# A transformer-style layer on one core: second parts of the query weights kept in DRAM between two groups of tokens, and the buffers of the dense expert pass laid out anew

## The chip, the cores and the metric

The kernel runs on one core of a Trainium2 chip. The metric is the time of one execution in microseconds (us) on the device. An engine is named as in the profile: PE is the matrix engine (TensorE), PEld its weight loads, DVE the vector engine, ACT the scalar engine, POOL GpSimd, and SP the sync engine, which here only issues DMAs. PEclk is the clock that PE was granted, as a share of its full speed.

## The reference, cut to what matters

One layer over 9 tiles of 128 tokens (one tile of context, eight of latent tokens), width 1024, all in fp32. Two mixers, an output projection and a gated residual come first. The part that the change touches is the last one, a product-key lookup over 128 x 128 single-neuron experts:

```
h = rmsnorm(x, norm2_g) * (1.0 + scale2) + shift2
q = (h @ w_q).reshape(n_tok, 8, 2, 128)            # 8 heads, two halves
s = einsum('thpc,hpkc->thpk', q, sub_keys)         # 128 scores per half
v1, i1 = top_k(s[:, :, 0], 16) ; v2, i2 = top_k(s[:, :, 1], 16)
top_v, top_j = top_k(v1[..., :, None] + v2[..., None, :], 16)
idx = i1 * 128 + i2 at top_j ; g = softmax(top_v)
a = gelu(einsum('bd,bed->be', h, u_tab[idx])) * g  # 128 experts per token
x = x + gate2 * einsum('be,bed->bd', a, v_tab[idx])
```

## The kernel before, in words

**Products.** A weight comes in units of 128 x 1024 floats (512 KB). `load_unit` (L147) loads one into a slot of `wraw` on SP's queue; `split` (L98) makes of it a first part `wH` (ACT, a rounded copy, L99) and a second part `wL` (DVE, the difference, L100). `mmx` (L124) then multiplies two such pairs with three matmuls: H by H (L129), H by L or L by H (L130, L131). `unit` (L181) does load and split in one; `wH` and `wL` have two buffers each.

**Stages.** After the mixers the latent tiles go in two groups of four through `group`: GA (tiles 5 to 8), then GB (tiles 1 to 4). A group does its output projection, the second norm, and then the *q stage*, a loop over 16 units of query weights (units 60 to 75 of the list, `u + 44 + b`): 24 matmuls `pq`, an ACT copy `qs`, four matmuls `psc` with the keys, and on DVE `top16` for each of the four tiles (L414 to L420: MAX, MAX_INDEX, MATCH_REPLACE, MAX, MAX_INDEX). Both groups read the same 16 units and split them again. When a group has its scores, `combine` chooses the 16 best pairs of each head.

**Two ways to use the experts.** Tiles 0 to 3 gather the rows of their experts: an indirect DMA on POOL's queue for each of 128 experts per token row (`gu`, `gv`), and a DVE instruction for each (`jk`, L814; `acc`, L829). Tiles 5, 6, 7, 8 and 4 (DENSE) take all experts in a dense pass. For that, a *build* turns a tile's choice into a matrix G in DRAM (`G_d`): one-hot rows on DVE and ACT, matmuls `pG`, ACT copies `Gs` (L563), writes by SP (L567). Tile 4 is in GB, so its choice and its build come last, directly ahead of the dense pass. The dense pass runs e over 128 groups of 128 experts: `hidden` (48 matmuls `pH` of 320 columns and a GELU on ACT) gives `a`; DVE multiplies `a` by a slice `Gt` of G (L1078) and splits it into `aH`, `aL`; `out_res` adds 18 matmuls `pout` for three tiles into PSUM; every fourth e `out_rot` does 48 matmuls `prot` for two tiles, added to `accd` on DVE. For each e a unit of u and one of v are loaded (`ur`, `vr`) and split. Group e's Gt comes for four e at a time, in five pieces, one for each tile.

**Order.** A scheduler lays the instructions of each engine out ahead of the run by priorities and by when buffers come free; every engine then runs its list in order. Work of the gather is let into DVE's list by `anchor` and `paced` (L104 to L114): a gather instruction may not stand ahead of the split that was recorded some units before. Ahead of the dense pass the two units u0 and u1 go through `unit` and their `pH` run before the build. Then the pools of the groups are closed and a pool `dp` is opened in their place, whose buffers (`raw`, `uH`, `uL`, `vH`, `vL`, `a`, `aH`, `aL`, `Gt`, `accd`) can be filled when what lay there before is done.

## Time and profile before

| | us |
|---|---|
| three runs | 3621.89, 3634.37, 3636.42; median 3634.37 |
| profiled execution, its own time | 3629.96 |
| span in the profile | 3628.2 |
| GA's q stage | about 940 to 1040 |
| GB's q stage, to the last top16 | about 1528 to 1657 |
| choice of tile 4, second half | 1657 to 1671.5 |
| build of tile 4 | 1671.5 to 1713 |
| dense pass | 1713 to 3606 |

The span is cut into stages by the names of the instructions. The profiled execution lies 4.4 us below the median of the three runs. PE is busy for 3336.8 us of the span, DVE for 2817.6, ACT for 1121.3, POOL for 1429.2. A busy share is an average over stages with different limits; the rows further below are taken stage by stage.

### The profile page before, as it was taken

Reading aid. Unit: us, or ns where it says so; the run is one execution under the profiler, and the core shown is the slowest. Engines: PE = TensorE matmul, PEld = TensorE weight load, DVE = VectorE, ACT = ScalarE, POOL = GpSimd, SP = SyncE. Lnnn points to the kernel's source line nnn. Section 1 sums busy time; section 2 is a strip of 40 time slices with the busy share of each in tenths; the row PEclk is TensorE's granted clock in tenths of the full one; section 3 lists DMA queues with packets and bytes.
Section 4 is the critical chain, followed back from the end, with each engine's and each line's share of the span. In section 5 each row is a group of like instructions: output and inputs, shape, how many; then the busy total and the mean of one; then the engine's idle time right before and its main releaser. Section 6 shows DMA issues by size and latency. Waiting matters only on the chain. (4 is left out here: it accounts for less than half of the span.)

```text
span 3628.2 us, 48825 instructions
## 1 busy us (share of the span) xinstructions
PE 3336.8 (92%) x17547; PEld 2764.3 (76%) x17547; DVE 2817.6 (78%) x5427; ACT 1121.3 (31%) x2095; POOL 1429.2 (39%) x1128
## 2 busy tenths in 40 slices
PE   8898999899887999877889999989999999999997
PEld 4386888775665676666788898889898888898996
DVE  2317678785899888697888888888887888788887
ACT  2512443321323655625322222222222222222222
POOL 0102102553112322200365664655555456555653
PEclk9899999999999999999999999999999999999998
DMA  7787324789534778643898997998998799988986
GB/s 282 287 294 274 113 72 132 257 313 342 168 127 141 271 255 325 248 144 117 291 332 299 326 327 268 336 326 306 324 319 320 245 343 333 324 305 316 337 320 247
DMA packets 361957, 971.12 MB, mean 268 GB/s; under 512 B 32721, under 2 KB 142673, under 8 KB 356081
## 3 DMA queue, kind: packets, MB, share of 16 engines
q0 software_dynamic: 149824, 546.37, 42.4%
q1 hardware_dynamic: 211888, 421.62, 33.6%
q8 instruction: 138, 2.26, 0.3%
q14 instruction: 107, 0.87, 0.1%
HBM read 897.07 MB, written 70.80 MB: 267 GB/s over the span
## 5 line engine op out<-in xcount | busy, mean ns | idle before, releaser
L811 POOL DMA_INDIRECT gu<-in_urow_dram,ix x512 | 688.2, 1344 | 1004.7 <-DVE jk L814 421.9
L824 POOL DMA_INDIRECT gv<-in_vrow_dram,ix x512 | 687.3, 1342 | 819.5 <-DVE acc L829 412.2
L814 DVE SCALAR_TENSOR_TENSOR jk<-gu,h2r 128x1024 f16<-128x1024 f32 x512 | 625.2, 1221 | 127.9 <-DMA gu<-in_urow_dram,ix 121.8
L829 DVE SCALAR_TENSOR_TENSOR acc<-gv,act,acc 128x1024 f32<-128x1024 f32 x508 | 651.3, 1282 | 45.2 <-DMA gv<-in_vrow_dram,ix 37.5
L129 PE MATMUL pH<-h2DH,uH 128*128 128x320 f32 x2016 | 626.5, 311 | 10.6 <-DVE accd L1061 8.2
L131 PE MATMUL pH<-h2DH,uL 128*128 128x320 f32 x2016 | 623.7, 309 | 1.1 <-DVE uL L100 1.1
L130 PE MATMUL pH<-h2DL,uH 128*128 128x320 f32 x2016 | 624.2, 310 | 0.0
L129 PEld LDWEIGHTS pH<-h2DH,uH 128*128 128x128 f32 x2016 | 380.4, 189 | 21.7 <-DVE accd L1061 13.4
L130 PEld LDWEIGHTS pH<-h2DL,uH 128*128 128x128 f32 x2016 | 380.4, 189 | 4.5
L131 PEld LDWEIGHTS pH<-h2DH,uL 128*128 128x128 f32 x2016 | 380.2, 189 | 1.7 <-DVE uL L100 1.7
L129 PE MATMUL pout<-vH,aH 128*128 128x512 f32 x768 | 300.6, 394 | 21.9 <-ACT vH L99 16.1
L99 ACT ACTIVATE vH<-vr 128x1024 fp32r<-128x1024 f32 x128 | 133.2, 1058 | 564.0 <-DMA vr<-in_vrow_dram 295.8
L131 PE MATMUL pout<-vH,aL 128*128 128x512 f32 x768 | 301.7, 393 | 4.1 <-DVE aL L100 4.1
L130 PE MATMUL pout<-vL,aH 128*128 128x512 f32 x768 | 301.7, 393 | 1.1 <-DVE vL L100 1.1
L129 PE MATMUL prot<-vH,aH 128*128 128x512 f32 x512 | 209.2, 409 | 54.4 <-DVE accd L1061 50.1
L99 ACT ACTIVATE wH<-wraw 128x1024 fp32r<-128x1024 f32 x118 | 124.9, 1058 | 401.9 <-PE pq L130 163.7
L100 DVE TENSOR_TENSOR vL<-vr,vH 128x1024 fp32r<-128x1024 f32 x128 | 156.1, 1220 | 91.0 <-ACT vH L99 90.9
L560 PE MATMUL pG<-oh 128*128 128x128 f16 x1280 | 176.8, 316 | 33.3 <-ACT Gs L563 21.6
L560 PEld LDWEIGHTS <-oh 128*128 128x128 f16 x1280 | 147.2, 131 | 78.0 <-issue 63.2
L130 PE MATMUL prot<-vL,aH 128*128 128x512 f32 x512 | 206.2, 403 | 0.0
L131 PE MATMUL prot<-vH,aL 128*128 128x512 f32 x512 | 205.5, 401 | 0.0
L99 ACT ACTIVATE aH<-a 128x640 fp32r<-128x640 f32 x128 | 94.2, 737 | 358.3 <-DVE a L1078 352.2
(345 smaller groups left out, 6306.4 us busy)
## 6 DMA issues: line engine op xcount, KB each, us to landing
wraw<-in_wst_dram SPq DMA_DIRECT2D x216, 512.0 KB, 4.6
vr<-in_vrow_dram SPq DMA_DIRECT2D x128, 512.0 KB, 6.8
ur<-in_ut_dram SPq DMA_DIRECT2D x126, 512.0 KB, 6.6
G_d<-Gs SPq DMA_DIRECT2D x40, 1024.0 KB, 5.0
Gt<-G_d SPq DMA_DIRECT2D x160, 256.0 KB, 9.6
wraw<-in_w_ada_dram SPq DMA_DIRECT2D x48, 512.0 KB, 5.5
gu<-in_urow_dram,ix POOLq DMA_INDIRECT x512, 6.7
gv<-in_vrow_dram,ix POOLq DMA_INDIRECT x512, 6.9
```

The lines of the kernel that those rows point to most:

```text
L99: A.activation(H, src, AF.Copy)
L100: return V.tensor_tensor(out=L, in0=src, in1=H.bitcast(F32), op=OP.subtract)
L129: P.matmul(ps, a[0], b[0], start=first, stop=False)
L130: P.matmul(ps, a[0], b[1], start=False, stop=False)
L131: P.matmul(ps, a[1], b[0], start=False, stop=last)
L560: P.matmul(pg[:, :, tt], oh[:, 0, :, tt], og[a][:, :, tt], start=(a == 0), stop=(a == 1))
L811: G.indirect_dma_start(out=ur, out_offset=None, in_=urow, in_offset=bass.IndirectOffsetOnAxis(ap=ix[:, c:c + 1], axis=0))
L814: paced(V.scalar_tensor_tensor(jk, ur, 1.0, h2r, op0=OP.mult, op1=OP.mult, accum_out=dots[:, k:k + 1]))
L824: G.indirect_dma_start(out=vr, out_offset=None, in_=vrow, in_offset=bass.IndirectOffsetOnAxis(ap=ix[:, c:c + 1], axis=0))
L829: paced(V.scalar_tensor_tensor(acc, vr, act[:, k:k + 1], acc, op0=OP.mult, op1=OP.add))
```

## The change

1. **Second parts through DRAM.** A buffer `wL_d` of units in DRAM is added. In GA's q stage SP writes each unit's `wL` there after the split. In GB's q stage ACT makes `wH` as before, but `wL` is read back from `wL_d` by a DMA on POOL's queue, and DVE does not subtract. As the splits were what the gather's work was anchored to, an anchor now stands on the last instruction of a tile's `top16`.
2. **The dense pass uses the slots of the weight stream.** The pool `wp` (`wraw`, `wH`, `wL`) stays open to the end. The units of u and v of the dense pass are loaded into `wraw`, those of u split into `wH`, `wL`. The other buffers of `dp` are laid out by a list (`order`), each with a slot of its own. The constants for the late choices (`cs32`) are loaded after those slots are laid out.
3. **First a in two pieces.** For e below 4 the multiplication by Gt and the split of `a` are done for the first four tiles (512 columns), then for tile 4 (128 columns).
4. The last step's `x1`, `ftmp` and two rows take other slots.

```diff
+KEPT = set(range(44, 60))
...
+    wL_d = dram.tile([60, 128, 1024], F32, name="wL_d")
...
-    wp = ph1.enter_context(tc.tile_pool(name="wp", bufs=2, side="right", reuse_waits="tile"))
+    wp = ctx.enter_context(tc.tile_pool(name="wp", bufs=2, side="right", reuse_waits="tile"))
...
         H = wp.tile([128, 1024], F32R, name="wH", bufs=2)
         L = wp.tile([128, 1024], F32R, name="wL", bufs=2)
+        if src is None and u - U_GR in KEPT and second[0]:
+            A.activation(H, raw, AF.Copy)
+            G.dma_start(L, wL_d[u - U_GR])
+            return [H, L]
         anchor(split(raw, H, L), 2)
+        if src is None and u - U_GR in KEPT:
+            nc.sync.dma_start(wL_d[u - U_GR], L.bitcast(F32))
         return [H, L]
...
-                top16(gp, pss[:, i * 128:(i + 1) * 128], tv[i][:, b // 2, b % 2, :], ti[i][:, b // 2, b % 2, :], 128)
+                ins = top16(gp, pss[:, i * 128:(i + 1) * 128], tv[i][:, b // 2, b % 2, :], ti[i][:, b // 2, b % 2, :], 128)
+                if i == 0 and tiles is GB:
+                    anchor(ins, 2)
...
+    second[0] = True
     group(gp, GB, hTBr, False)
...
+    R5 = [128, D], F32R
+    SLOTS = {"Gt": ([128, TD // TB, GI, TB], F32), "accd": ([128, D], F32),
+             "vH": R5, "vL": R5, "aH": ([128, TD], F32R), "aL": ([128, TD], F32R), "a": ([128, TD], F32)}
+    first = {}
+
+    def slot(name, i=0):
+
+        if (name, i) in first:
+            return first.pop((name, i))
+        return dp.tile(*SLOTS[name], name=name, tag=f"{name}{i}", bufs=1)
+    order = ["Gt0", "vH2", "vL2", "Gt1", "accd0", "accd1", "grow", "vH3", "vL3", "aH4",
+             "vH0", "vL0", "vH1", "vL1", "aH0", "aL0", "aH1", "aL1", "a0",
+             "aH2", "aL2", "aH3", "aL3", "aL4", "a1", "vH4", "vL4"]
+    held = []
+    for x in order:
+        if x == "grow":
+            rows_of[:] = [(dp, NGD)]
+            held = [row("cs32") for _ in range(NGD)]
+            C["coff"], C["clen"], C["cj"] = load_cs3(dp, held[0])
+        else:
+            first[x[:-1], int(x[-1])] = slot(x[:-1], int(x[-1]))
...
-    C["coff"], C["clen"], C["cj"] = load_cs3(dp, row("cs32"))
-
...
-    def load_split(src, nm, bufs):
-        raw = dp.tile([128, 1024], F32, name=nm + "r", tag="raw", bufs=3)
-        nc.sync.dma_start(raw, src)
-        H, L = [dp.tile([128, 1024], F32R, name=nm + z, bufs=bufs) for z in "HL"]
+    def load_split(src, H, L):
+        raw = load_unit(src, False)
         fill(split(raw, H, L))
         return H, L
...
-            ab = a.rearrange("p (b t) -> p b t", t=TB)
-            V.tensor_tensor(out=ab, in0=ab, in1=Gt[:, :, e % GI, :], op=OP.mult)
-            aH, aL = [dp.tile([128, TD], F32R, name="a" + z, bufs=GI + 1) for z in "HL"]
-            fill(split(a, aH, aL))
+            aH, aL = [slot("a" + z, e % (GI + 1)) for z in "HL"]
+
+            for b0, b1 in ((0, RES + 1), (RES + 1, ND)) if e < GI else ((0, ND),):
+                t = slice(b0 * 128, b1 * 128)
+                ab = a[:, t].rearrange("p (b t) -> p b t", t=TB)
+                V.tensor_tensor(out=ab, in0=ab, in1=Gt[:, b0 * 128 // TB:b1 * 128 // TB, e % GI, :], op=OP.mult)
+                ins = split(a[:, t], aH[:, t], aL[:, t])
+            fill(ins)
             if 0 < e < 127:
-                u = load_split(ut[e + 1], "u", 2)
-            v = load_split(vt[e], "v", GI + 1)
+                u = load_split(ut[e + 1], *[wp.tile([128, 1024], F32R, name="w" + z, bufs=2) for z in "HL"])
+            v = load_split(vt[e], *[slot("v" + z, e % (GI + 1)) for z in "HL"])
```

How this moves the lists of the engines, at three places. A row is the line, the operation, out<-in and the shape; x2 stands for two alike in a row.

POOL, from GB's second norm to the end of its q stage (`gv` are gathered rows, `ss` and `rstd` the norm, `h2DH` and `h2DL` the two 2.5 MB loads that the dense pass needs). Before:

```order
L824 DMA gv<-in_vrow_dram,ix_2105 128x1024 x11
L256 TENSOR_TENSOR ss_11573<-ss_11573 128x1
L824 DMA gv<-in_vrow_dram,ix_2105 128x1024
L94 TENSOR_SCALAR rstd<-ss_11573 128x1
L256 TENSOR_TENSOR ss_11584<-ss_11584 128x1
L824 DMA gv<-in_vrow_dram,ix_2105 128x1024
L95 TENSOR_TENSOR rstd<-rstd,nhalf 128x1
L94 TENSOR_SCALAR rstd<-ss_11584 128x1
L256 TENSOR_TENSOR ss_11595<-ss_11595 128x1
...
L990 DMA h2DH<-h2T_d 128x5120
L990 DMA h2DL<-h2T_d 128x5120
L824 DMA gv<-in_vrow_dram,ix_2105 128x1024 x3
```

Now:

```order
L194 DMA wL<-wL_d 128x1024
L836 DMA gv<-in_vrow_dram,ix_2106 128x1024 x5
L194 DMA wL<-wL_d 128x1024
L836 DMA gv<-in_vrow_dram,ix_2106 128x1024 x4
L266 TENSOR_TENSOR ss_11590<-ss_11590 128x1
L96 TENSOR_SCALAR rstd<-ss_11590 128x1
L97 TENSOR_TENSOR rstd<-rstd,nhalf 128x1
...
L194 DMA wL<-wL_d 128x1024 x2
L1003 DMA h2DH<-h2T_d 128x5120
L194 DMA wL<-wL_d 128x1024
L836 DMA gv<-in_vrow_dram,ix_2106 128x1024
L194 DMA wL<-wL_d 128x1024
```

The four norm steps stand together, with the gathered rows ahead of them; the reads of `wL` stand among `gv`, `h2DH` and `h2DL` on the one queue that POOL issues from.

SP, from the last writes of the choices of tiles 1 to 3 (`tvi_d`) to the first a (`cs_13787` is `cs32`). Before:

```order
L769 DMA tvi_d<-tv 128x256
L769 DMA tvi_d<-ti 128x256
L567 DMA G_d<-Gs 128x2048 x8
L1070 DMA Gt<-G_d 128x4x128 x5
L789 DMA late<-tvi_d 128x512
L1038 DMA vr<-in_vrow_dram 128x1024
L1038 DMA ur<-in_ut_dram 128x1024
L1038 DMA vr<-in_vrow_dram 128x1024
```

Now:

```order
L781 DMA tvi_d<-tv 128x256
L781 DMA tvi_d<-ti 128x256
L158 DMA wraw<-in_ut_dram 128x1024
L158 DMA wraw<-in_vrow_dram 128x1024
L158 DMA wraw<-in_ut_dram 128x1024
L158 DMA wraw<-in_vrow_dram 128x1024
L577 DMA G_d<-Gs 128x2048 x8
L893 DMA cs_13787<-in_small_dram 128x768
L1102 DMA Gt<-G_d 128x4x128 x5
L801 DMA late<-tvi_d 128x512
L158 DMA wraw<-in_ut_dram 128x1024
```

Four loads of u and v moved ahead of the writes of G, and the load of `cs32` now stands between the last of these and the first Gt.

DVE, at the end of tile 4's build (`oh` are its one-hot rows, `a_13022` or `a_13039` the a of e = 0, the other that of e = 1). Before:

```order
L532 TENSOR_TENSOR oh<-iota,rt 128x1024
L540 TENSOR_TENSOR oh<-oh,gl 128x512
L542 TENSOR_TENSOR oh<-oh,gl 128x512
L882 CAST cs_13774<-cs_13773 128x768
L1078 TENSOR_TENSOR a_13022<-a_13022,Gt 128x640
L1078 TENSOR_TENSOR a_13081<-a_13081,Gt 128x640
```

Now:

```order
L542 TENSOR_TENSOR oh<-iota,rt 128x1024
L550 TENSOR_TENSOR oh<-oh,gl 128x512
L552 TENSOR_TENSOR oh<-oh,gl 128x512
L102 TENSOR_TENSOR vL<-wraw,vH 128x1024 x2
L894 CAST cs_13789<-cs_13787 128x768
L102 TENSOR_TENSOR vL<-wraw,vH 128x1024
L1114 TENSOR_TENSOR a_13039<-a_13039,Gt 128x512
L1114 TENSOR_TENSOR a_13098<-a_13098,Gt 128x512
L1114 TENSOR_TENSOR a_13039<-a_13039,Gt 128x128
L102 TENSOR_TENSOR aL<-a_13039,aH 128x512
```

Three splits of v moved ahead of the first product with Gt, and that product comes in pieces of 512 and 128 columns. On PE, 73 matmuls `pH` (e = 2 and half of e = 3) stand between the last `pG` and the first `pout`, where before the first `pout` followed `pG` at once.

## Rows read from the trace of the kernel before

**Rows 1.** The page: the busy time of each engine over the span.

```profile
PE 3336.8 (92%) x17547; PEld 2764.3 (76%) x17547; DVE 2817.6 (78%) x5427; ACT 1121.3 (31%) x2095; POOL 1429.2 (39%) x1128
```

**Rows 2.** Stretches of the span: start:end, length, then for each engine its busy us and (instructions), then PEclk, the DMA engines' mean busy share, GB/s. In order: GB's q stage, the build of tile 4, what follows the build up to the first `pout`, the first three e, the stretch from the first gathered row on, the rest of the dense pass.

```profile
1529.00:1657.00 128.00, 105.99 (x501) 84.87 (x499) 116.77 (x601) 28.48 (x39) 6.73 (x7) 0.92 0.42 146
...
1671.50:1712.00 40.50, 33.60 (x247) 27.80 (x248) 37.66 (x84) 36.87 (x124) 0.00 (x0) 0.96 0.38 156
1712.00:1729.40 17.40, 1.29 (x13) 0.98 (x10) 3.53 (x14) 3.76 (x8) 0.00 (x0) 0.65 0.91 296
1729.40:1761.00 31.60, 30.52 (x152) 26.86 (x153) 31.11 (x105) 14.30 (x18) 0.60 (x1) 0.87 0.67 200
1761.00:1915.00 154.00, 135.31 (x721) 121.35 (x720) 124.00 (x156) 31.86 (x48) 98.53 (x74) 0.95 0.95 332
1915.00:3605.70 1690.70, 1633.35 (x9018) 1476.09 (x9016) 1418.00 (x1863) 418.72 (x613) 950.88 (x703) 0.98 0.89 314
```

**Rows 3.** What PE waited for from 1525 to 1657 us: waiting instruction, releaser, total us, times, longest.

```profile
PE pq L131 <- DVE wL L100: 16.8, 2, 10.1
```

**Rows 4.** ACT's timeline in GB's q stage, the copy of each unit's scores: start, us, engine, line, operation, out<-in.

```profile
1528.62 0.58 ACT L757 ACTIVATE qs<-pq 128x512 f32<-128x512 f32 x1
...
1588.73 0.58 ACT L757 ACTIVATE qs<-pq 128x512 f32<-128x512 f32 x1
...
1608.66 0.58 ACT L757 ACTIVATE qs<-pq 128x512 f32<-128x512 f32 x1
...
1621.26 0.58 ACT L757 ACTIVATE qs<-pq 128x512 f32<-128x512 f32 x1
...
1638.47 0.58 ACT L757 ACTIVATE qs<-pq 128x512 f32<-128x512 f32 x1
```

**Rows 5.** DVE's groups in the same stage: busy us, mean ns | idle before and releaser.

```profile
L100 DVE TENSOR_TENSOR wL<-wraw,wH 128x1024 fp32r<-128x1024 f32 x16 | 19.3, 1213 | 9.5 <-ACT wH L99 9.5
...
L829 DVE SCALAR_TENSOR_TENSOR acc<-gv,act,acc 128x1024 f32<-128x1024 f32 x7 | 8.9, 1272 | 0.0
```

**Rows 6.** PE's timeline there: two matmuls in a row at full clock, and two behind the second stall.

```profile
1539.11 0.40 PE L129 MATMUL pq<-h2H,wH 128*128 128x512 f32 x1
1539.34 0.39 PE L130 MATMUL pq<-h2L,wH 128*128 128x512 f32 x1
...
1630.73 0.63 PE L130 MATMUL pq<-h2L,wH 128*128 128x512 f32 x1
1631.15 0.63 PE L131 MATMUL pq<-h2H,wL 128*128 128x512 f32 x1
```

**Rows 7.** POOL's timeline in the same stage: how long an issue holds POOL.

```profile
1532.32 0.64 POOL L990 DMA_DIRECT2D h2DH<-h2T_d  x1 [29.73 <-issue]
...
1548.15 1.95 POOL L824 DMA_INDIRECT gv<-in_vrow_dram,ix  x1 [13.39 <-DVE tv L419]
```

**Rows 8.** DMA issues: queue, count, KB each, median us from issue to landing.

```profile
wraw<-in_wst_dram SPq DMA_DIRECT2D x216, 512.0 KB, 4.6
...
G_d<-Gs SPq DMA_DIRECT2D x40, 1024.0 KB, 5.0
...
gv<-in_vrow_dram,ix POOLq DMA_INDIRECT x512, 6.9
...
h2DH<-h2T_d POOLq DMA_DIRECT2D x1, 2560.0 KB, 10.0
h2DL<-h2T_d POOLq DMA_DIRECT2D x1, 2560.0 KB, 16.0
```

**Rows 9.** A stretch in the middle of GA's q stage, columns as in rows 2.

```profile
960.00:1000.00 40.00, 38.83 (x190) 31.17 (x189) 39.44 (x201) 9.27 (x12) 5.60 (x4) 1.00 0.41 140
```

**Rows 10.** POOL's timeline in GB's second norm.

```profile
1494.31 1.89 POOL L824 DMA_INDIRECT gv<-in_vrow_dram,ix  x1 [0.22 <-DVE acc L829]
1496.27 0.19 POOL L94 TENSOR_SCALAR rstd<-ss 128x1 f32<-128x1 f32 x1
...
1496.87 0.98 POOL L824 DMA_INDIRECT gv<-in_vrow_dram,ix  x1
```

**Rows 11.** SP's timeline at the end of tile 4's build.

```profile
1684.82 29.69 SPq L567 DMA_DIRECT2D G_d<-Gs  x8
1714.60 6.76 SPq L1070 DMA_DIRECT2D Gt<-G_d  x5
```

**Rows 12.** PE's timeline: the last matmuls of the build, and the first `pout` with the idle time ahead of it.

```profile
1711.31 1.97 PE L560 MATMUL pG<-oh 128*128 128x128 f16 x16 [0.28 <-ACT Gs L563]
...
1729.38 2.93 PE L129 MATMUL pout<-vH,aH 128*128 128x512 f32 x6 [16.11 <-ACT vH L99]
```

**Rows 13.** PE's timeline a little later: two matmuls `pH` in a row at full clock.

```profile
1745.01 0.31 PE L131 MATMUL pH<-h2DH,uL 128*128 128x320 f32 x1
1745.16 0.31 PE L129 MATMUL pH<-h2DH,uH 128*128 128x320 f32 x1
```

**Rows 14.** DVE's timeline: the first product with Gt, with the idle time ahead of it.

```profile
1726.05 1.56 DVE L1078 TENSOR_TENSOR a<-a,Gt 128x640 f32<-128x640 f32 x2 [13.87 <-DMA Gt<-G_d]
```

**Rows 15.** DVE's timeline: the first gathered row of the dense pass.

```profile
1769.02 1.23 DVE L814 SCALAR_TENSOR_TENSOR jk<-gu,h2r 128x1024 f16<-128x1024 f32 x1 [5.36 <-DMA gu<-in_urow_dram,ix]
```

**Rows 16.** What PE waited for from 1761 to 1915 us.

```profile
PE prot L129 <- DVE accd L1061: 14.5, 2, 9.2
```

**Rows 17.** What DVE waited for in that stretch.

```profile
DVE jk L814 <- DMA gu<-in_urow_dram,ix: 17.6, 6, 5.4
```

More of the change, by code (lines that the diff above doesn't have):

```diff
@@ L142, in hybrid_kernel @@
     ph1 = ExitStack()
-    wp = ph1.enter_context(tc.tile_pool(name="wp", bufs=2, side="right", reuse_waits="tile"))
+    wp = ctx.enter_context(tc.tile_pool(name="wp", bufs=2, side="right", reuse_waits="tile"))
     nload = [0]
+    second = [False]
     def load_unit(src, native=True):
@@ L419, in top16 @@
         V.max(v_[:, 8:16], m[:, :n])
-        V.max_index(i_[:, 8:16], v_[:, 8:16], m[:, :n])
+        return V.max_index(i_[:, 8:16], v_[:, 8:16], m[:, :n])
     def combine(gp, t, tv, ti, al=None, c4=None, V=V, h0=0, h1=8, res=None):
@@ L1011, in hybrid_kernel @@
     dp = ctx.enter_context(tc.tile_pool(name="dp", bufs=1, side="right", reuse_waits="tile"))
+    R5 = [128, D], F32R
[17 more added lines that the diff above has]
+            first[x[:-1], int(x[-1])] = slot(x[:-1], int(x[-1]))
     po = [[pmm("pout") for _ in range(2)] for _ in range(RES)]
-    accd = [dp.tile([128, D], F32, name=f"accd{i}") for i in range(ROT)]
+    accd = [slot("accd", i) for i in range(ROT)]
     vt = vrow.rearrange("(e p) d -> e p d", p=128)
     late_q = deque(combine_late(t) for t in late)
-    C["coff"], C["clen"], C["cj"] = load_cs3(dp, row("cs32"))
     nrow[0] = 0
@@ L1066, in hybrid_kernel @@
             if e % GI == 0:
-                Gt = dp.tile([128, TD // TB, GI, TB], F32, name="Gt", bufs=2)
+                Gt = slot("Gt", e // GI % 2)
                 for z in range(ND):
@@ L1074, in hybrid_kernel @@
             else:
-                a = dp.tile([128, TD], F32, name="a", bufs=2)
+                a = slot("a", e % 2)
                 hidden(a, u)
-            ab = a.rearrange("p (b t) -> p b t", t=TB)
-            V.tensor_tensor(out=ab, in0=ab, in1=Gt[:, :, e % GI, :], op=OP.mult)
-            aH, aL = [dp.tile([128, TD], F32R, name="a" + z, bufs=GI + 1) for z in "HL"]
-            fill(split(a, aH, aL))
+            aH, aL = [slot("a" + z, e % (GI + 1)) for z in "HL"]
[5 more added lines that the diff above has]
+            fill(ins)
             if 0 < e < 127:
-                u = load_split(ut[e + 1], "u", 2)
-            v = load_split(vt[e], "v", GI + 1)
+                u = load_split(ut[e + 1], *[wp.tile([128, 1024], F32R, name="w" + z, bufs=2) for z in "HL"])
+            v = load_split(vt[e], *[slot("v" + z, e % (GI + 1)) for z in "HL"])
         if e > 0:
@@ L1090, in hybrid_kernel @@
             grp.append((e, aH, aL, *v))
-    gt2 = dp.tile([128, D], F32R, name="gt2d", tag="vH", bufs=GI + 1).bitcast(F32)
+    gt2 = slot("vH", 128 % (GI + 1)).bitcast(F32)
     nc.sync.dma_start(gt2, gate_d[3:4, :].to_broadcast([128, D]))
-    fgd = dp.tile([128, D], F32R, name="fgd", tag="vH", bufs=GI + 1).bitcast(F32)
+    fgd = slot("vH", 129 % (GI + 1)).bitcast(F32)
     nc.sync.dma_start(fgd, fng[None].to_broadcast([128, D]))
     for i in range(ND):
-        dst = accd[i - RES] if i >= RES else dp.tile([128, D], F32R, name="ftmp", tag="vL", bufs=GI + 1).bitcast(F32)
-        x1 = dp.tile([128, D], F32, name="x1", tag="raw", bufs=3)
+        dst = accd[i - RES] if i >= RES else slot("vL", (128 + i) % (GI + 1)).bitcast(F32)
+        x1 = wp.tile([128, D], F32, name="x1", tag="wraw", bufs=3)
         final(dp, DENSE[i], dst, po[i] if i < RES else [dst], x1, gt2, fgd)
```

## The prediction

> **What bounds the kernel now.** I read the page first, to see that PE is busy for 92% of the span and so most of any gain must come from places where it stands still [rows 1]. Then the span cut into stretches, to find these places [rows 2]. Two matter here. In GB's q stage PE is busy for 106.0 of 128 us, DVE for 116.8. Behind tile 4's build PE is busy for 1.3 of 17.4 us. The dense pass from 1915 us on has PE at 1633.4 of 1690.7 us, and the change leaves its work as it is.
>
> The waits of PE in the q stage name the cause: two waits, 16.8 us, for DVE's `wL` [rows 3]. ACT's copies of the scores show it as a rhythm: one unit every 6.68 us where nothing is late (1528.62 to 1588.73 is nine units), then gaps of 19.93 and 17.21 us [rows 4]. So 13.2 and 10.5 us, together 23.8, are lost to late splits and to the clock behind them: a matmul takes 0.42 us behind the second stall instead of 0.23 [rows 6].
>
> **Part 1, GB's q stage.** DVE loses 14 of the 16 subtractions that it does there (units 0 and 1 are read ahead of the stage in the new list; the two subtractions that remain are those of u0 and u1): 14 x 1.21 = 16.9 us [rows 5]. By the new list it gets two more gathered rows, 2 x 1.27 = 2.5. Its work is then 116.8 - 14.4 = 102.4 of what was 128 us. PE at its undisturbed rhythm saves 23.8. Both ends agree: the stage can become at most some 24 us shorter.
>
> Against that stands the new trip. `wL` has two buffers, so the read for unit i may start when PE is done with unit i-2, and PE is on unit i-1 for 6.68 us meanwhile. If release to landing takes T, each of 14 units waits T - 6.68. No row shows such a read, so it is bounded: 512 KB on SP's queue land in 4.6 us, gathered rows of the same size on POOL's queue in 6.9 [rows 8]; a gathered row issued just ahead holds POOL for up to 1.95 [rows 7]. T lies between 4.6 and 8.9, the loss between 0 and 31 us. I take 6.9 as the nearest row (the same queue and size): 14 x 0.2 = 3. Two reads are dearer: `h2DH` and `h2DL`, 2.5 MB each, which landed 10.0 and 16.0 us after issue [rows 8], stand on the same queue ahead of the reads for units 4 and 6; some 2 us each beyond the slack, so 4. The part gives -24 + 7 = -17 (from -24 to +7). What ends the stage after it, the choice and build of tile 4, hangs on the last scores and moves with it in full.
>
> What would undo this is an issue that is held up. Here an issue took 0.64 us for `h2DH` and 1.95 for a row, in a stage in which DVE was busy for 91% of the time [rows 2, 7]. The Trainium skill, "SBUF — State Buffer", section "A bandwidth-pool intuition that's wrong (but worth ruling out)", says that a DMA issued by GpSimd takes about 620 ns alone and about 3100 ns beside a DVE copy, since its descriptors wait for a port that DVE holds. The row of 0.64 speaks against it here, the row of 1.95 leaves it possible; by the page's two figures the sum of this part would be an estimated -17 + 14 x 2.5 = +18.
>
> In GA's q stage SP gets one write of 512 KB ahead of each load. SP waits there for the same subtraction that frees the slot for its load, and the DMA engines are 41% busy [rows 9]; DVE and PE do the same as before. A load lands in 4.6 us and has 6.68, so that one issue more, at 0.64 as on POOL [rows 7, 8], finds cover; without it 16 x 0.64 = 10 would be the price. From 0 to +3, +1 as a value.
>
> **Part 1, GB's second norm.** Before, gathered rows stood between the four norm steps on POOL, two of them 1.89 + 0.98 us long [rows 10]. In the new list the rows stand ahead and the steps run together. Up to -3, or 0 if the rows ahead are themselves late: -1.
>
> **Part 2, tile 4's build.** The split of u3 moves into it, and part of that of u2: one more ACT copy and one more subtraction in 40.5 us, in which ACT is busy 36.9 and DVE 37.7 [rows 2]. From 0 to 2 x 1.2, I take +1.
>
> **Parts 2 and 3, from the build to the dense pass.** Before, PE's last `pG` ends at 1713.3, and the first `pout` starts at 1729.38, 16.11 us later [rows 12]. The reason: SP issues G's writes until 1714.5, then the first Gt pieces until 1721.4 [rows 11], and DVE stands 13.87 us until Gt lands [rows 14]. Now u2 and u3 are loaded and split ahead, so PE has 73 `pH` in this gap, 73 x 0.147 = 10.7 us [rows 13], and does not come out of it at a lowered clock (mean 0.65 in the gap [rows 2]). Gt itself does not come sooner: its issue still waits for the last write of G to land (5.0 us [rows 8]), and the load of `cs32` now stands ahead of it on SP: 0 to +1. With Gt as one transfer for each tile, the piece for tile 4 is the last, and the four others wait in the same queue for the same writes, so I give the two pieces of a nothing beyond two or three more instructions for each of four e (+1), which DVE has room for only where it waits.
>
> What is late next is DVE: from 1729.4 to 1761 it is busy for 31.1 of 31.6 us [rows 2]. Three splits of v and two of u leave this stretch, 5 x 1.21 = 6 us, of which 1 goes back to the pieces. Then the gathered rows start; the first `jk` had waited 5.36 us for its row [rows 15]. From 1761 to 1915 the DMA engines are 95% busy at 332 GB/s, DVE waits 17.6 us for rows [rows 17], and PE waits 14.5 us for `accd`, which DVE adds late [rows 16]. PE's 10.7 us ahead are worth their full price only if PE is what ends last there; as the gather and the weights both go through the DMA engines, a part is taken back. Bounds: 0 (all given back) and -13 (PE's 10.7 and two for the clock). I take DVE's number, -6 with rounding, as it is the engine that is full in the next stretch. From e = 13 on the lists of both kernels hold the same number of gathered rows.
>
> **Part 4** renames slots at the end: 0.
>
> **Sum.** -17 + 1 - 1 + 1 - 6 = -22. The profiled execution took 3629.96, so 3608 in its like; the median lay 4.4 above it, so 3612 as a median.
>
> **The rivals.**
>
> *A, PE-limited start.* The DMA share of 0.95 from 1761 on was work that PE had asked for late, and PE keeps its lead. The transition gives -13: 3605. For it: PE waits only 14.5 us there for DVE. Against it: DVE waits for rows 17.6 us in the same stretch [rows 16, 17].
>
> *B, the lead is given back.* From 1761 on the transfers set the pace and the transition gives 0: 3618. For it: 332 GB/s there, more than the 314 of the stretch after [rows 2].
>
> *C, the issues are held up.* While DVE is busy, POOL needs 1.95 us for an issue as for the longer row [rows 7], and the landing takes 6.9 behind that: T = 8.85, 14 x 2.17 = 30, so the stage is 6 longer than before in place of 17 shorter, and the transition alone is left: 3612 + 17 + 6 = 3635. For it: the stage has DVE busy without a pause. Against it: 0.64 for `h2DH` in the same stage. The Trainium skill's two figures, from the section named above, would make T an estimated 6.9 + 2.5 = 9.4 us.
>
> *D, slower.* The same mechanism past its point: POOL issues in order, and reads behind `h2DH`, `h2DL` and rows that wait for DVE come so late that PE also falls to its half clock (0.42 for 0.23 us [rows 6]). At T = 9.3 the stage is 14 x 2.62 - 24 = 13 us longer; half clock on a third of a unit's 24 matmuls, 8 x 0.19 = 1.5 us, makes 21 more over 14 units. Together 13 + 21 - 5 = +29: 3663. The point from which the kernel is slower than before is where 14 x (T - 6.68) passes 24 + 5, T of 8.75, just inside the bound of 8.9.
>
> *E, it does not do what it says.* The second parts come back in time, but DVE's list in the q stage fills with other work (combine, rows) and the stage keeps its length. The list speaks against it: two rows more, no other work.
>
> **How the numbers follow.** What can be told from no change is about 0.5%, 18 us: faster is below 3616, slower above 3652. Forecast (3605 to 3618, most of it below 3616) 0.48, A 0.14 (it reaches down to 3593 with no loss on the trip), B 0.14 (half of it below 3616), C 0.12, D 0.07, E 0.05 (3630). Faster: 0.40 + 0.14 + 0.07 = 0.61, with some of C and E that ends lower 0.03 more, 0.64. Slower: D and 0.01 of C, 0.08. Same: what is left, 0.28. The range takes in the forecast, A with no loss on the trip (3605 - 7, and 8 for the scatter of single runs), B and E, and stops at the edge of C: 3590 to 3634, which leaves out D, most of C and little else, 0.18.
>
> **What would show it.** In GB's q stage: no PE wait on DVE's `wL`; in its place waits on the DMA of `wL`, in sum 0 to 10 us; copies of scores every 6.7 us; the last `top16` some 17 us earlier; DVE near 102 us. If PE waits for the DMA of `wL` over 24 us in sum, part 1 is wrong. In the transition: `pH` without a gap behind `pG`, the first Gt product at the same distance from the end of the build as now (12 to 13 us), and the first `jk` some 6 us nearer to the build. If PE's lead of some 11 us is still whole at 1915, A holds; if gone, B. What would make the whole wrong is a stretch that I cost at nothing: GA's q stage with SP's writes, or the dense pass, in which a shift of 1% is 18 us.

## The result, and the profile after

The changed kernel took 3606.05 us (median of 7 runs, 3600.18 to 3614.76), the kernel before 3635.91 beside it (7 runs). The ratio is 0.9932, 95% interval 0.9919 to 0.9944: 30 us less. The prediction said 3612, 3590 to 3634.

The profiled execution of the changed kernel was its slowest: 3614.76 us, span 3613.0. Against the span before, 3628.2, that is only 15 us. Where the other 15 are is read below by distances inside each trace, since some stretches ahead of GB's q stage differ between executions whose lists there are the same.

The page, busy times, to be set against [rows 1]:

```profile
PE 3338.7 (92%) x17547; PEld 2764.6 (77%) x17547; DVE 2800.7 (78%) x5419; ACT 1121.6 (31%) x2099; POOL 1433.0 (40%) x1144
```

Stretches as in [rows 2] (GB's q stage to the last top16; the build; the gap behind it; the first e; from the first gathered rows; the rest). The bounds moved with the work:

```profile
1541.00:1652.50 111.50, 100.50 (x485) 80.70 (x485) 104.54 (x594) 27.96 (x37) 15.22 (x22) 0.96 0.71 247
...
1668.00:1709.00 41.00, 34.09 (x247) 27.98 (x248) 38.25 (x84) 37.64 (x125) 0.00 (x0) 0.96 0.41 167
1709.00:1729.00 20.00, 13.77 (x88) 13.11 (x87) 7.18 (x18) 7.22 (x14) 0.00 (x0) 0.89 0.74 256
1729.00:1761.00 32.00, 32.00 (x161) 27.79 (x161) 30.30 (x114) 11.24 (x18) 2.57 (x3) 0.96 0.68 202
1761.00:1895.00 134.00, 119.78 (x644) 107.17 (x643) 115.91 (x144) 29.81 (x43) 93.01 (x70) 0.95 0.97 353
1895.00:3590.00 1695.00, 1634.29 (x9011) 1475.54 (x9009) 1422.70 (x1870) 418.62 (x613) 952.59 (x705) 0.98 0.89 314
```

The q stage is 111.5 us long, and DVE is busy for 104.5 of it: DVE is what ends it now. In the gap PE has 13.8 us of work where it had 1.3, and from 1761 on the DMA engines move 353 GB/s, more than the 332 that looked like a limit in [rows 2].

What PE waited for in GB's q stage, 1537 to 1655 us, to be set against [rows 3]:

```profile
PE pH L131 <- DVE mrep L428: 6.9, 2, 3.8
PE pq L133 <- DMA wL<-wL_d: 2.0, 2, 1.6
```

ACT's copies of the first and the last unit's scores, as in [rows 4], 100.0 us apart:

```profile
1540.25 0.58 ACT L767 ACTIVATE qs<-pq 128x512 f32<-128x512 f32 x1
...
1640.26 0.58 ACT L767 ACTIVATE qs<-pq 128x512 f32<-128x512 f32 x1
```

POOL's issues of the second parts in the same stage, to be set against [rows 7]; two of them with a gathered row between:

```profile
1573.31 0.53 POOL L194 DMA_DIRECT2D wL<-wL_d  x1 [6.05 <-PE pq L133]
1574.15 1.49 POOL L836 DMA_INDIRECT gv<-in_vrow_dram,ix  x1 [0.30 <-issue]
...
1581.18 0.57 POOL L194 DMA_DIRECT2D wL<-wL_d  x1 [4.26 <-PE pq L133]
```

SP behind the build, to be set against [rows 11], and then DVE there, against [rows 14]:

```profile
1681.31 31.54 SPq L577 DMA_DIRECT2D G_d<-Gs  x8
1718.16 0.33 SPq L893 DMA_DIRECT2D cs<-in_small_dram  x1
1718.55 2.88 SPq L1102 DMA_DIRECT2D Gt<-G_d  x5
```

```profile
1721.50 0.56 DVE L894 CAST cs<-cs 128x768 f16<-128x768 f32 x1 [7.20 <-DMA cs<-in_small_dram]
...
1725.87 1.50 DVE L1114 TENSOR_TENSOR a<-a,Gt 128x512 f32<-128x512 f32 x3 [2.68 <-DMA Gt<-G_d]
```

PE there, against [rows 12]: the first `pout` has 6.2 us of idle time ahead of it in place of 16.1, and the 73 `pH` stand between.

```profile
1708.29 1.96 PE L570 MATMUL pG<-oh 128*128 128x128 f16 x16 [0.29 <-ACT Gs L573]
...
1727.28 0.80 PE L131 MATMUL pout<-vH,aH 128*128 128x512 f32 x1 [6.23 <-ACT aH L101]
```

**The distances.** Each is taken from the start times of the rows named, in us, within one trace. A: first to last `qs` of GB's q stage. B: last `qs` to the end of the last top16. C: from there to the last `Gs` row of the build (a pair of copies). D: last `Gs` to the fourth `accd` (the first four e are done). E: last `Gs` to the sixteenth `accd`. F: last `Gs` to the end of the span. "Ahead" is the last `qs` of GA to the first of GB.

| | ratio to before (95% interval) | ahead | A | B | C | D | E | F |
|---|---|---|---|---|---|---|---|---|
| before | 1 | 490.5 | 122.4 | 7.2 | 55.1 | 77.8 | 261.4 | 1914.9 |
| changed | 0.9932 (0.9919 to 0.9944) | 497.7 | 100.0 | 12.2 | 57.8 | 61.9 | 242.8 | 1902.7 |
| e1 relay alone | 0.9971 (0.9959 to 0.9982) | 499.1 | 100.3 | 12.2 | 55.8 | 77.6 | 258.6 | 1911.7 |
| e2 dense part alone | 0.9975 (0.9963 to 0.9986) | 493.1 | 122.7 | 7.1 | 57.5 | 61.3 | 242.9 | 1908.2 |
| e3 cs32 after Gt | 0.9934 (0.9920 to 0.9949) | 491.2 | 100.3 | 12.2 | 57.8 | 60.4 | 242.3 | 1903.6 |
| e4 a in one piece | 0.9954 (0.9940 to 0.9968) | 496.1 | 99.9 | 12.2 | 58.0 | 61.7 | 252.6 | 1916.9 |
| e5 wL read twice | 1.0019 (1.0006 to 1.0032) | 496.6 | 139.3 | 10.8 | 56.8 | 60.5 | 240.6 | 1898.2 |
| e6 pieces for e = 0, 1 | 0.9927 (0.9906 to 0.9949) | 496.4 | 100.5 | 12.2 | 56.1 | 59.1 | 241.3 | 1903.9 |
| e7 u2, u3 split late | 0.9984 (0.9970 to 0.9999) | 496.8 | 100.1 | 12.2 | 55.3 | 80.6 | 264.6 | 1925.7 |
| e8 three moves | 0.9958 (0.9945 to 0.9972) | 504.3 | 100.5 | 9.8 | 56.0 | 61.1 | 243.2 | 1902.7 |
| e9 one row for cs32 | 0.9920 (0.9899 to 0.9941) | 493.3 | 101.7 | 12.2 | 57.3 | 61.4 | 245.3 | 1900.1 |
| e10 as e9, cs32, u3 | 0.9904 (0.9880 to 0.9928) | 496.6 | 102.0 | 12.2 | 55.8 | 61.5 | 243.0 | 1907.5 |
| e11 wL by SP | 0.9956 (0.9942 to 0.9971) | 495.8 | 111.1 | 12.1 | 57.5 | 62.5 | 246.5 | 1904.8 |
| e12 one piece, one row | 0.9933 (0.9912 to 0.9953) | 495.5 | 100.2 | 12.2 | 56.2 | 62.6 | 255.5 | 1911.2 |

So in the changed kernel the q stage (A + B) is 17.4 us shorter, the build 2.7 longer, the first four e are done 15.9 sooner behind it, sixteen e 18.6 sooner, and 12.2 of that reach the end. Together that is 26.9 us. The spans differ by 15.2 only, as the changed trace is 11.7 us longer ahead of these distances: 4.5 up to GA's first `qs` (936.64 and 941.09 us) and 7.2 in "ahead". D flatters the change: up to the fourth `accd` DVE has done 12 gathered rows behind the build before, 4 now; at the sixteenth both have done the same number.

### The profile page after: what moved, and what is told of

It is laid out like the page before. It is cut to its first block, busy times and chain, and to the rows that moved or that the text cites. A ratio compares the mean times of both kernels' runs of the same rounds, so it can differ in the third digit from the quotient of the medians.

```text
span 3613.0 us, 48879 instructions
## 1 busy us (share of the span) xinstructions
PE 3338.7 (92%) x17547; PEld 2764.6 (77%) x17547; DVE 2800.7 (78%) x5419; ACT 1121.6 (31%) x2099; POOL 1433.0 (40%) x1144
## 5 line engine op out<-in xcount | busy, mean ns | idle before, releaser
L131 PE MATMUL pH<-h2DH,wH 128*128 128x320 f32 x2048 | 635.9, 310 | 12.6 <-DVE mrep L428 6.9
L133 PE MATMUL pH<-h2DH,wL 128*128 128x320 f32 x2048 | 634.3, 310 | 2.0 <-DVE wL L102 2.0
L132 PE MATMUL pH<-h2DL,wH 128*128 128x320 f32 x2048 | 633.6, 309 | 0.0
L101 ACT ACTIVATE wH<-wraw 128x1024 fp32r<-128x1024 f32 x228 | 241.3, 1058 | 552.9 <-PE pH L132 201.0
L131 PEld LDWEIGHTS pH<-h2DH,wH 128*128 128x128 f32 x2048 | 385.9, 188 | 23.0 <-DVE mrep L428 7.5
L132 PEld LDWEIGHTS pH<-h2DL,wH 128*128 128x128 f32 x2048 | 385.9, 188 | 4.4
L133 PEld LDWEIGHTS pH<-h2DH,wL 128*128 128x128 f32 x2048 | 385.6, 188 | 3.2 <-DVE wL L102 3.2
L102 DVE TENSOR_TENSOR wL<-wraw,wH 128x1024 fp32r<-128x1024 f32 x228 | 278.0, 1220 | 62.1 <-ACT wH L101 58.1
L101 ACT ACTIVATE vH<-wraw 128x1024 fp32r<-128x1024 f32 x128 | 133.6, 1060 | 605.1 <-DMA wraw<-in_vrow_dram 303.1
L102 DVE TENSOR_TENSOR vL<-wraw,vH 128x1024 fp32r<-128x1024 f32 x128 | 156.1, 1221 | 88.0 <-ACT vH L101 85.4
```

Of the source, the lines that this page charges most:

```text
L101: A.activation(H, src, AF.Copy)
L102: return V.tensor_tensor(out=L, in0=src, in1=H.bitcast(F32), op=OP.subtract)
L131: P.matmul(ps, a[0], b[0], start=first, stop=False)
L132: P.matmul(ps, a[0], b[1], start=False, stop=False)
L133: P.matmul(ps, a[1], b[0], start=False, stop=last)
```

## The experiments

**e1 and e2: the two parts apart.** In e1 the change's first part on the kernel before, in e2 the changed kernel without it:

```diff
+        if src is None and u - U_GR in KEPT and second[0]:
+            A.activation(H, raw, AF.Copy)
+            G.dma_start(L, wL_d[u - U_GR])
+            return [H, L]
...
+            nc.sync.dma_start(wL_d[u - U_GR], L.bitcast(F32))
```

```diff
-KEPT = set(range(44, 60))
+KEPT = set()
...
-                if i == 0 and tiles is GB:
-                    anchor(ins, 2)
```

> The kernel before with part 1 alone (second parts of the query weights through DRAM, anchors on top16); the dense pass and its buffers as before. Theory (the relay is worth the shorter q stage, the dense part its own lead): scores of GB's q stage every 6.6 us, about 100 us from first to last qs in place of 122.4, the last top16 some 17 us nearer to the first qs than before; ratio to before about 0.995 (-17 us), with 0.9965 if the tail of top16 on DVE takes a part. Rival 1 (the dense part gives nothing, all of the gain is the relay's): 0.993. Rival 2 (what follows the stage swallows it): 0.999 or more.

> The changed kernel without part 1: query weights split twice as before, no relay, no anchors on top16; the dense pass on the weight stream's slots, laid out anew, first a in two pieces. Theory (PE's 73 pH in the gap behind the build stay a lead): ratio about 0.997 (-10 us), e = 13 reached 10 to 13 us sooner after the last pG than before. Rival 1 (the lead is given back to the transfers): 1.000. Rival 2 (the two parts need each other): the two runs alone sum to clearly less than the 0.0068 of both.

Measured: 0.9971 and 0.9975, about 10 and 9 us; together 0.0054 of the 0.0068 of both, within the intervals. Of the two runs, the q stage is short only in e1 (112.5 us against 129.6), D and E only in e2. Each part has its own mechanism, and neither swallows the other. Of e1's 16 us at the build's end, 10 are seen in the time; its "ahead" was 499.1, to which I come back.

**e3: cs32 behind the first Gt.**

```diff
-            C["coff"], C["clen"], C["cj"] = load_cs3(dp, held[0])
...
+                if e == 0:
+                    C["coff"], C["clen"], C["cj"] = load_cs3(dp, held[0])
```

> The changed kernel with one thing moved: the load of cs32 is issued after the first Gt pieces, not ahead of them. Theory (cs32 waits on SP 5.1 us for G's last write to land and holds the four Gt pieces that need not wait): first Gt issue about 4 to 5 us sooner after G's last write, first product with Gt 3 to 5 us sooner after the last pG, ratio about 0.992 (3 to 4 us under the changed kernel). Rival (the landing of Gt is set by what else is on the DMA engines, or by the piece for tile 4): first product at the same distance of 15.6 us, ratio 0.993.

SP's timeline in e3:

```profile
1674.31 31.64 SPq L577 DMA_DIRECT2D G_d<-Gs  x8
1706.04 5.44 SPq L1101 DMA_DIRECT2D Gt<-G_d  x5
1711.59 0.63 SPq L893 DMA_DIRECT2D cs<-in_small_dram  x1
```

Gt is now issued right behind the last write of G, and the first product with it starts 12.1 us behind the last `Gs` in place of 15.6. In the eight other traces with `cs32` ahead of Gt this distance is 14.0 to 15.8, in the two others with it behind (e8, e10) 13.4: the wait was real, at some 2 us in the mean. But the fourth `accd` comes 1.5 sooner, the sixteenth 0.5, and the time is the same. Both theories were half right: the product comes sooner, and little of that reaches the end. That PE's `pH` cover it is argued.

**e4 and e6: the first a in pieces.** e4 drops the pieces, e6 keeps them for e = 0 and 1:

```diff
-            for b0, b1 in ((0, RES + 1), (RES + 1, ND)) if e < GI else ((0, ND),):
+            for b0, b1 in ((0, ND),):
```

```diff
-            for b0, b1 in ((0, RES + 1), (RES + 1, ND)) if e < GI else ((0, ND),):
+            for b0, b1 in ((0, RES + 1), (RES + 1, ND)) if e < 2 else ((0, ND),):
```

> The changed kernel with the first four a multiplied and split in one piece of 640 columns, as before. Theory (with cs32 ahead of all Gt, the piece for tile 4 lands right with the others): no difference beyond 2 us, ratio 0.993. Rival (the two pieces let the first aH come earlier and so the first pout): 2 to 4 us slower than the changed kernel, 0.994.

> The changed kernel with only the a of e = 0 and e = 1 in two pieces, those of e = 2 and 3 in one. Theory (the pieces count where PE has nothing left to do, in the first pout; the one-piece run lost its 9 to 11 us in e = 4 to 7, where its list has one gathered row more ahead of accd and that row came late): as the changed kernel, 0.993, since the list has the same rows ahead of accd as the changed kernel. Rival (every one of the four pieces counts): halfway, 0.9943 or more.

e4 lost 8 us to the changed kernel (the two intervals just meet), e6 nothing. The loss does not come where the pieces are: D is 61.7 and 61.9. It comes in the next four e, which took 76.2 us for 65.2. PE's waits in e4 there (1766 to 1845 us), and DVE's:

```profile
PE prot L131 <- DVE accd L1093: 13.7, 1, 13.7
```

```profile
DVE jk L826 <- DMA gu<-in_urow_dram,ix: 8.3, 3, 5.9
```

e4's list on DVE has 36 gathered rows ahead of the first `accd` of these four e, the changed kernel's and e6's 35; within these four e alone 33 and 31. DVE works in order, so an `accd` behind a row that has not landed keeps PE waiting, and in that stretch PE's mean clock fell to 0.89 from 0.95. e12, below, has 36 rows again.

**e5: every second part read twice.**

```diff
             G.dma_start(L, wL_d[u - U_GR])
+            G.dma_start(L, wL_d[u - U_GR])
```

> The changed kernel with every second part read twice, one read right behind the other into the same buffer, so that the trip is longer by one issue of about 0.55 us and by the time of 512 KB more. Theory (the trip was covered, with little to spare: PE waited 2.0 us in sum where it has 6.57 us for each): the trip becomes 2 to 3 us longer, PE waits 0 to 2 us for each of 14 units, the distance from first to last qs goes from 100 to 105 to 125 us, ratio 0.995 to 1.001. Rival (the trip has much to spare, so held-up issues would have cost nothing either): distance 100 to 102, ratio 0.993. Rival of the prediction (POOL's issues are held up while DVE works): an issue of 2 us or more, distance above 125.

A is 139.3 us, and the kernel is 0.2% slower than before. A distance above 125 was to be the sign of held-up issues; the issues themselves took 0.53 to 0.63 us. PE's waits in the stage, then POOL's timeline, then the issues with their landing:

```profile
PE pq L133 <- DMA wL<-wL_d: 23.4, 11, 6.4
```

```profile
1600.37 0.54 POOL L195 DMA_DIRECT2D wL<-wL_d  x1 [4.73 <-DMA wL<-wL_d]
1601.29 0.53 POOL L194 DMA_DIRECT2D wL<-wL_d  x1 [0.39 <-PE pq L133]
1608.22 0.53 POOL L195 DMA_DIRECT2D wL<-wL_d  x1 [6.40 <-DMA wL<-wL_d]
```

```profile
wL<-wL_d POOLq DMA_DIRECT2D x32, 512.0 KB, 5.1
wL_d<-wL SPq DMA_DIRECT2D x16, 512.0 KB, 2.9
```

The second read waits until the first has landed (both write one buffer), so the trip is not 2 to 3 us longer, as I had expected, but twice as long, about 0.5 + 4.7 + 5.1 = 10.3 us. A landing takes 5.1 us. PE's waits grow from 2.0 to 23.4. The rest of the 39 is mostly the clock: the mean granted clock between the first and the last `qs` is 0.90 where the changed kernel has 1.00, and matmuls take 0.43 to 0.44 us in the mean for 0.40, an estimated 13 us over 384 of them. By the median a single trip has 1.0 to 1.5 us to spare (6.6 less 5.1, and the issue of 0.5 if the 5.1 does not hold it), a double one has not.

**e7: the splits of u2 and u3 behind the first product with Gt.** `behind` puts an instruction behind a marked one in its engine's list.

```diff
+        h = A.activation(H, raw, AF.Copy)
+        ins = V.tensor_tensor(out=L, in0=raw, in1=H.bitcast(F32), op=OP.subtract)
+        if late_u:
+            late_u.pop(0)
+            behind(h, marks["aH"][:1])
+            behind(ins, marks["a"][:1])
```

> The changed kernel with one order forced: u2 and u3 are loaded early as now, but split only behind the first product with Gt, so that PE has no pH in the gap behind the build. Theory (the lead is the 73 pH): PE stands some 14 us behind the last pG, the fourth accd comes 74 to 78 us after the last Gs in place of 62, ratio 0.997 (as the relay alone). Rival (the splits of v, taken out of DVE's full stretch, gave the lead): fourth accd within 66 us, ratio 0.994 or less.

The first `pout` in e7:

```profile
1716.24 0.79 PE L131 MATMUL pout<-vH,aH 128*128 128x512 f32 x1 [15.41 <-ACT aH L1131]
```

The gap is back, D is 80.6, and the whole lead is gone, with two of the three splits of v still early. So there is no lead without the 73 `pH`, and the early splits of v alone give none. Whether they add to it where PE has its `pH` was not tried; the splits of u2 and u3 went back together with the `pH`.

**e8: three moves.** cs32 as in e3; u3's split behind the build; `RATE[2]` from 0.5 to 0.7, so that 9 gathered rows and not 12 are left in GB's q stage.

```diff
-RATE = (1.5, 2.6, 0.5, 2.5, 6.1, 4.5)
+RATE = (1.5, 2.6, 0.7, 2.5, 6.1, 4.5)
...
+            behind(h, marks["Gs"])
+            behind(ins, marks["oh"])
```

> The changed kernel with three things moved: cs32 loaded after the first Gt; u3 split behind the build and not within it; and the gather a little faster ahead of GB's q stage, so that 9 rows and not 12 are left in it. Theory (DVE ends the q stage now, and the build is held by u3's split): last top16 about 4 us nearer to the first qs, last Gs 2 us nearer to the last top16, ratio 0.991 to 0.992. Rival (each is given back in the dense pass): 0.993.

What was aimed at came: B is 9.8, C 56.0, so the build's end is 3.7 us nearer to the first `qs`. But the three rows went ahead of the stage, where the distance "ahead" is 504.3, the longest of all, and the time is 9 us above the changed kernel's. It looks as if DVE's work was moved from one full stretch into another; three rows are 3.8 us, and the rest of the 9 is not explained. B with three rows of 1.27 us less is 2.4 us shorter, which bears out that B is DVE's.

**e9 and e10: the phase of the rows.** The lead shrinks from 18.6 us at sixteen e to 12.2 at the end. Times of a group of four e, fourth `accd` to fourth `accd` (the first four e are group 0), show where: groups 8, 18 and 19 took 73.0, 61.4 and 73.2 us before, 76.1, 66.3 and 79.3 in the changed kernel; the same in e2 (77.8, 66.7, 78.0), not in e1 (72.1, 60.9, 72.2). In these a choice of a gathered tile runs on DVE (`late`). The gathered rows go round a list of six slots, and the change takes two of them for cs32 where one was taken, so all later rows are in another slot.

```diff
-            held = [row("cs32") for _ in range(NGD)]
+            held = [row("cs32")]
```

e10 adds to this line e3's move and e8's two lines `behind`, u3's split behind the build.

> The changed kernel with one row and not two taken when cs32 is laid out. The rows of the gather go round a list of six slots, so this puts them back in the phase that they had before, and DVE's list of e = 16 to 123 is then that of the kernel before. Theory (the changed kernel loses some 14 us of its lead in the groups of four e where a late choice runs, 8, 18 and 19, which took 76.1, 66.3 and 79.2 us for 73.0, 61.4 and 73.2 before, by the phase of the rows): these groups as before, the dense pass from the last Gs to the end 10 to 14 us shorter than the 1902.7 of the changed kernel, ratio 0.989 to 0.991. Rival (the loss comes with the weight stream's slots or the other buffers, not with the phase): the groups stay long, ratio 0.993.

> As the run before, and cs32 loaded after the first Gt, and u3 split behind the build. Theory: the build about 2 us shorter (56 from the last top16 to the last Gs in place of 57.8), the fourth accd 1 us sooner, so 0 to 4 us under the run with one row, ratio 0.988 to 0.991. Rival (what is won there is lost in the first e): as that run.

The three groups went back to 72.6, 61.4 and 72.6 in e9, 73.2, 61.2 and 71.5 in e10. The ends of group 18 and 19 on DVE, in the changed kernel and then in e9:

```profile
2838.69 0.68 DVE L1093 TENSOR_TENSOR accd<-accd,prot 128x512 f32<-128x512 f32 x1
...
2917.94 0.68 DVE L1093 TENSOR_TENSOR accd<-accd,prot 128x512 f32<-128x512 f32 x1
```

```profile
2828.46 0.68 DVE L1093 TENSOR_TENSOR accd<-accd,prot 128x512 f32<-128x512 f32 x1
...
2901.08 0.68 DVE L1093 TENSOR_TENSOR accd<-accd,prot 128x512 f32<-128x512 f32 x1
```

What happens in group 18 can be read from the waits. In the changed kernel DVE stands for the load of a choice's scores (`late`), and PE then for `accd`; in e9 DVE has no such wait, and PE's is short. DVE's and PE's waits in that group in the changed kernel, then PE's in e9:

```profile
DVE late L121 <- DMA late<-tvi_d: 4.6, 1, 4.6
```

```profile
PE prot L131 <- DVE accd L1093: 6.0, 1, 6.0
```

```profile
PE prot L131 <- DVE accd L1093: 1.3, 1, 1.3
```

SP issues that load behind the five pieces of Gt in the changed kernel, ahead of them in e9; SP in the changed kernel, then in e9:

```profile
2807.30 5.59 SPq L1102 DMA_DIRECT2D Gt<-G_d  x5
2813.62 1.24 SPq L801 DMA_DIRECT2D late<-tvi_d  x1
```

```profile
2798.56 0.33 SPq L801 DMA_DIRECT2D late<-tvi_d  x1
...
2801.75 5.35 SPq L1102 DMA_DIRECT2D Gt<-G_d  x5
```

It is so in every trace. In the five of the old phase the load is issued ahead of Gt, 13.2 to 13.4 us before DVE first uses it, and DVE does not wait. In the nine of the new phase it is issued behind Gt, DVE stands 3.9 to 4.9 us for it, PE 4.4 to 6.4 for `accd` (0.4 to 1.3 in the old phase), and PE's mean clock in the group is 0.92 to 0.97 for 1.00. The `late` tile takes a slot of the rotation, so its load can come no sooner than that slot is free. In group 19 the longest wait of DVE for a gathered row is 4.2 to 5.7 us in the new phase, 1.8 to 2.6 in the old.

So the phase costs 14 us in these three groups, as expected. It does not give 14 in the whole: other groups are shorter in the changed kernel's phase (group 14: 58.2 for 60.2, group 20: 51.7 for 53.9). Groups 4 to 30 take 1582.6 to 1593.4 us in the five traces of the old phase, mean 1585.7, and 1587.8 to 1594.9 in the nine of the new, mean 1590.5. So the forecast for e9 was missed: F is 2.6 us shorter and not 10 to 14, and the ratio 0.9920 and not 0.991 or less. By the time, e9 has a median of 3602.98 and e10 of 3598.19, the lowest of all; both intervals still meet the changed kernel's, so no gain in time is shown. e10's distances are those of its slowest run, 3610.26. Its C is 55.8, 2 us shorter than the changed kernel's, as expected; but e6 and e12, with u3's split within the build, have 56.1 and 56.2.

**e11: the second parts by SP's queue.**

```diff
-            G.dma_start(L, wL_d[u - U_GR])
+            nc.sync.dma_start(L.bitcast(F32), wL_d[u - U_GR])
```

> The changed kernel with the second parts read back on SP's queue and not on POOL's. Theory (the trip is landing time and hardly the issue, which is 0.53 us on POOL and 0.33 on SP): distance from first to last qs 100 to 102 us, ratio 0.993. Rival 1 (POOL's queue was the dear part of the trip): PE's waits for wL vanish, distance 99. Rival 2 (on SP the reads stand behind loads that wait for their slots): PE waits, distance above 105, ratio 0.995 or more.

```profile
PE pq L133 <- DMA wL<-wL_d: 8.2, 2, 4.1
```

A is 111.1, and two reads came late. The number is the second rival's, its reason is not: SP issued both as soon as PE had freed their slots. PE's two waits and the two issues that they belong to:

```profile
1546.13 0.80 PE L133 MATMUL pq<-h2H,wL 128*128 128x512 f32 x1 [4.12 <-DMA wL<-wL_d]
...
1559.14 0.80 PE L133 MATMUL pq<-h2H,wL 128*128 128x512 f32 x1 [4.09 <-DMA wL<-wL_d]
```

```profile
1534.26 0.32 SPq L194 DMA_DIRECT2D wL<-wL_d  x1
...
1542.04 0.33 SPq L194 DMA_DIRECT2D wL<-wL_d  x1
```

So these reads were under way for some 12 and 17 us. In this time POOL's queue moved `h2DH` and `h2DL`, 2.5 MB each, issued at 1533.61 and 1544.76, and from 1540 to 1555 the DMA engines had a share of 1.00 or more and moved 387 to 445 GB/s. In the changed kernel the engines are as full there (428 and 413 GB/s from 1545 to 1555), but the reads stand between these two loads in POOL's one list, the two are issued 13.7 us apart, and PE's waits are 0.4 and 1.6. That the reads on another queue had to share the engines with `h2DH` and `h2DL` fits, but was not tried by itself.

**e12: e9 with all a in one piece.** e9's line and e4's:

```diff
-            held = [row("cs32") for _ in range(NGD)]
+            held = [row("cs32")]
...
+            for b0, b1 in ((0, ND),):
```

> The run with one row for cs32, and all a in one piece. Its list has 36 gathered rows ahead of the first accd of the second group of four e, as the one-piece run had, where the kernels with pieces have 35. Theory (the one-piece run lost 10 us there because accd stands behind one row more, and that row came late): the second group takes 70 us or more in place of 65, ratio 6 to 10 us worse than the run with one row. Rival (that loss was an accident of one run's profile and the pieces are worth 2 us at most): second group 65 to 67 us, ratio within 0.001 of that run.

The second group took 74.6 us (e4 76.2, changed 65.2), with 36 rows ahead of its first `accd`: the loss of e4 comes again with its list. But e9, with 35 rows ahead of the first and 36 of the second `accd` as the changed kernel has, took 70.4. So the count of rows ahead does not give the loss to the microsecond. By the time e12 is 5 us above e9 in the ratio, within both intervals.

## Why the prediction was right

The sum was -22, the median moved by 30. Point by point:

**GB's q stage, -17 predicted, -17.4 measured (A + B).** The mechanism was right; that the size fits is luck, as two terms were off and cancel. The trip was to cost 7: T was taken as 6.9 from gathered rows on POOL's queue. It landed in 5.1 (the median in e5, where the trace has it), nearer to the other bound of 4.6, and PE waited 2.0 in sum, 1.6 of it for a read issued behind `h2DH`. So A fell by 22.4, close to the 23.8 that PE had lost. In its place stood what the prediction counted but did not add: DVE's 102.4 us of work, 104.5 in the trace, ends the stage, and B grew by 5.0.

**The held-up issue (C), and D.** In a stage in which DVE was busy for 104.5 of 111.5 us, POOL's issues of `wL` took 0.53 to 0.63. The Trainium skill, "SBUF — State Buffer", section "A bandwidth-pool intuition that's wrong (but worth ruling out)", describes a DMA issued by GpSimd that waits beside a DVE copy. The issues here show nothing of it, but they are no test of it either: most of DVE's time in the stage is MAX8, FIND_INDEX8 and MATCH_REPLACE8 (the five large groups make 90.9 us), and copies and casts make 0.4. D's point was shown by e5 instead: with T of about 10.3, beyond the 8.75 named, the stage is 20.5 us longer than before and the kernel 0.2% slower, with PE's clock part of it.

**GA's q stage, +1.** From first to last `qs` 101.5 us both times (936.64 to 1038.12, 941.09 to 1042.58): 0.

**GB's second norm, -1.** From ACT's copy of the q stage's first unit, which is split ahead of the norm, to that of its third 76.2 us before and 76.0 after, 75.9 to 78.4 in the other runs with the relay (e8, which moves rows, left out): 0 to +2. The rows that stood between the norm steps were no loss.

**The build, +1.** +2.7 in the one trace. C is 56.1 to 58.0 in the eight traces of the changed kernel and its variants with u3's split within the build, 56.0 and 55.8 in the two with it behind (e8, e10), 55.1 in the kernel before: a cost of some 1 to 2 us in the mean, so +1 was fair, and part of the 2.7 is scatter.

**The transition, -6.** This is the step that failed in size. I took DVE's room, as DVE was full in the next stretch, and named PE's lead as rival A (-13). It was A, and more at first: 18.6 us at the sixteenth `accd`, where both lists have done the same gathered rows, and e7 shows that without the `pH` there is no lead. The 12.2 at the end is near A's 13 only since the phase of the rows, which A did not reckon with, takes some 5 back. The lead is larger than the 10.7 of the `pH` by the clock: a mean of 0.96 where it had been 0.87 in the stretch up to 1761, 0.09 x 32 = an estimated 3 us; the rest, some 5, was not taken apart. The row that misled was the DMA share of 0.95 with 332 GB/s [rows 2], read as a limit; with PE ahead the same engines moved 353. DVE's waits for rows [rows 17] fit latency behind slots that DVE itself frees better than a full DMA: in that stretch of the kernel before, POOL could not issue rows until DVE was done with others, here for `gv`.

```profile
POOL gv L824 <- DVE acc L829: 15.7, 9, 5.3
```

Gt came no sooner, as predicted, and later by 2.8, where 0 to 1 was given for `cs32`.

**The pieces of a.** "Nothing beyond more instructions" was right for the stretch in which they stand and for e6. e4 cost 8 us all the same, through the list behind them.

**The dense pass, "0".** It is not 0: the phase of the rows costs 14 us in three groups and gives back about 9 in others, some 5 in sum that the prediction put at nothing without a reason. Here lay the danger that the prediction named, "a shift of 1% is 18 us", without its cause: the number of slots that one line takes.

**What stays open.** "Ahead" is 490.5 and 493.1 in the two traces without the relay, 491.2 to 499.1 in the eleven with it (e8, which moves rows, left out), though the lists are alike up to the first unit's copy; whether the relay costs some 4 us there or this is scatter was not settled. e3, which has the relay, stands at 491.2. In the phase of the rows the wait for `late` explains group 18; groups 8 and 19, and what the other groups win, were not followed to a cause.

## What to carry to other kernels

A gap in which the busiest engine stands still can be worth its length if that engine is given later work of its own there, and the way to see whether the lead lasts is to follow one instruction that comes once in each round to the end, not the stretch behind the gap. A buffer trip that is covered by one round of the loop is nearly free up to that length and costs waits and clock past it, so measure its landing and not only its waits. And a change that lays buffers out anew may shift a rotation far behind it: compare the time of each round before and after, and where some rounds differ, look for the slot count, and for a load that has to wait for its slot.

## What the runs showed of the hardware that was not expected

POOL's issue of a 512 KB read took 0.53 to 0.63 us with DVE 94% busy, and in e5 the read landed in 5.1 us (median), where gathered rows of that size on the same queue had taken 6.9. In this program two reads into one buffer go one after the other: the second issue waited 4.7 and 6.4 us for the first to land. And DMA engines that showed a share of 0.95 at 332 GB/s moved 353 GB/s at 0.97 in the same stretch of the changed kernel.
